# A two-layer decoder trunk with experts: one room for staged weights, fixed places for side work, a shorter split queue, and a router without GpSimd

## The chip, the cores and the metric

The kernel runs on one core of a Trainium2 chip. The metric is the time of one execution on the device in microseconds (us). Five engines work beside each other, each through its own instructions in the order in which they were written: PE (TensorE, matmuls), DVE (VectorE), ACT (ScalarE), POOL (GpSimd) and SP (SyncE, which here only issues loads). They wait for each other by semaphores. Sixteen DMA engines move the data.

## The reference

Two pre-norm layers over 256 tokens of width 1024. Each layer is an attention block and a feed-forward block; the feed-forward is a dense SwiGLU in layer 0 and a mixture of 8 experts, two for each token, in layer 1. A last RMS norm follows. All is float32.

```python
def swiglu(t, w_gate, w_up, w_down):
    return (jax.nn.silu(t @ w_gate) * (t @ w_up)) @ w_down

def moe_swiglu(h, router, w_gate, w_up, w_down):
    ...
    logits = (t @ router).astype(jnp.float32)
    top_val, top_idx = lax.top_k(logits, TOP_K)
    gates = jax.nn.softmax(top_val, axis=-1)
    combine = jnp.sum(jax.nn.one_hot(top_idx, N_EXPERTS, dtype=jnp.float32) * gates[..., None], axis=1)
    out = jnp.zeros_like(t)
    for e in range(N_EXPERTS):
        out = out + combine[:, e:e + 1].astype(t.dtype) * swiglu(t, w_gate[e], w_up[e], w_down[e])
    return out.reshape(B, S, D)
```

Each expert has three matrices of 1024 x 3584 values: 44 MB in float32, 352 MB for the eight. Each is read once.

## The kernel before

**Weights in a stream.** All weights come through one class, Stream, as a list of units in the order of use. SP loads a unit in float32 into a stage tile (load_next, L162). ACT casts it into a float16 tile, its high part `hi` (L169, scaled by 512). DVE makes the low part `lo` = stage * 512 - hi, also float16 (L172). PE then makes three float16 products: hi with the high part and the low part of the tokens, and lo with their high part. A few units are marked to be used unsplit, in float32 (L1151); each gate and each up matrix of a half ends with one. There are nine stage tiles and six pairs of hi and lo, and four more places for a stage in tiles that attention leaves free. A stage is free when its low part is made, and the next load is issued then (low_done, L192 to L199). At most eight loads are under way. The stream splits up to six units ahead of the one in use (`most`), and the split instructions are written into ACT's and DVE's order at that place.

**Experts in halves.** An expert is worked in two halves of 1792 hidden columns, 16 halves i = 0 to 15. For a half, gate_up takes 8 gate units and 8 up units of 128 x 1792 (28 or 42 matmuls each, of 128 x 96), and then the chain that makes the hidden values: for each of three column ranges, DVE multiplies silu(gate) by up (sg, L1178), ACT casts (L1179), DVE subtracts (L1180). Then down takes the 7 down units (2 x 128 rows of 1024 columns each) of the half before, i - 1. So the order of the units is gate(i), up(i), down(i-1). The last down half is split finer at its end, and its last nine units are split in two halves each (`brisk`).

**Side work.** Before an expert, its tokens (at most 96) are put in columns: slots (DVE, L1070) makes the selection, four gathers (PE L1082, then xgh by ACT and xgl by DVE L1087) and gather_last fetch them. After an expert, turn_back (L1210 to L1216) and scatter (L1218 to L1224) add its result to x. These pieces are taken from a queue, one after each up unit from the sixth on and after each down unit.

**The router.** At the end of attention of layer 1, the residual is added (x, L736). Then Plain.part squares x on ACT and multiplies it by the norm's gain on POOL (L440, four operations), PE makes the logits, DVE finds the two largest and the row scale y from the squares (L357 to L362). hh is the high part of x * gain * y, hl its low part (L1108). SP goes on issuing the experts' loads meanwhile, as far as stages are free. top_up (L1114) is called once in the middle of this and casts the next unit.

**The end.** After the last down half: finish (L1208), turn_back, scatter into x (L1224), the last norm and the output (L1265).

Of the kernel before, what the change touches and what calls it, by code (L numbers as in the profile page):

```python
# [41 lines left out]
NB = FH // P  # L42

# [26 lines left out]
def hybrid_trunk_kernel(ctx: ExitStack, tc: tile.TileContext, a: dict, out: bass.AP, dbg=None):  # L70
# [4 lines left out]
    stgp = ctx.enter_context(tc.tile_pool(name="stgp", bufs=N_STG))  # L75
    cvtp = ctx.enter_context(tc.tile_pool(name="cvtp", bufs=N_CVT))
# [30 lines left out]
    def expert_units(sets, tail=False):  # L107
# [3 lines left out]
        for i in range(len(seq) + 1):  # L111
# [4 lines left out]
            if i > 0:  # L116
                (_, _, wd), h = seq[i - 1]
                ends = tail and i == len(seq)
                got += [(rows(wd, h * FH + r * P, 2, 0, D), 2, D, False) for r in range(0, NB - 4 if ends else NB, 2)]
                if ends:  # L120
                    r0 = h * FH + (NB - 4) * P
                    got += [(rows(wd, r0 + r * P, kt, c0, 512), kt, 512, False) for r, kt, c0 in ((0, 4, 0), (0, 2, 512), (2, 2, 512))]
        return got

    MLA_KT = (2, 2, 4)
    units = []
    for layer in range(DEPTH):
# [12 lines left out]
        else:  # L140
            sets = [(a["moe_w_gate"][j, e], a["moe_w_up"][j, e], a["moe_w_down"][j, e]) for e in range(NE)]
            units += expert_units(sets, layer == DEPTH - 1)

    class Stream:


        def __init__(self, units, stage_tile, part_tiles, ahead):
            self.units, self.stage_tile, self.part_tiles = units, stage_tile, part_tiles
            self.loaded = self.split = self.low = self.used = 0
            self.stage, self.place, self.high, self.ready = {}, {}, {}, {}  # L150
# [3 lines left out]
            self.brisk = 0  # L154

        def load_next(self, place=None):
            u = self.loaded
            if u < len(self.units):
                src, kt, n, _ = self.units[u]
                stg = self.stage_tile(u, place)  # L160
                self.place[u] = place
                nc.sync.dma_start(stg[:, : kt * n].rearrange("p (k n) -> p k n", k=kt), src)  # L162
                self.stage[u] = stg
                self.loaded += 1
            elif place is None and self.last:
                self.last.pop()()
# [7 lines left out]
        def split_next(self):  # L174
# [7 lines left out]
            m = self.units[u][1] * self.units[u][2]  # L182
            self.high[u] = self.part_tiles[0](u)
            self.split += 1
            if u >= len(self.units) - self.brisk:
                self.low_until(u)
                lo = self.part_tiles[1](u)
# [8 lines left out]
        def top_up(self):  # L196

            if self.split < min(len(self.units), self.used + N_CVT) and not self.units[self.split][3]:
                u = self.split  # L199
                self.high[u] = self.part_tiles[0](u)  # L200
# [21 lines left out]
        def get(self, later=0):  # L222
            while self.split <= self.used + later:
                self.split_next()
# [1178 lines left out]
```

## Time and profile before

| | us |
|---|---|
| three runs | 1367.33, 1368.21, 1368.56 |
| median | 1368.21 |
| profiled execution | 1368.37 |
| its span | 1366.6 |
| first expert matmul | 495.03 |
| output issued | 1357.48 |

The span is what the trace covers; the execution's own time is 1.8 us longer. All times in the rows below are us from the start of the span. A row of the timeline gives start, duration, engine, line, operation, what it writes and reads, how many were merged, and in brackets the idle time of the engine before it with what ended it.

### The profile page before, as it was taken

The numbers are of one execution on the slowest core, as the hardware profiler recorded it, in microseconds if no ns is written. First come the engines' busy times: TensorE is split into PE (matmuls) and PEld (weight loads), VectorE is DVE, ScalarE is ACT, GpSimd is POOL, SyncE is SP. The second block draws the span as 40 slices with busy tenths as digits, with TensorE's granted clock in tenths as the row PEclk, the third lists the DMA queues.
The fourth block names the chain that finished last, engine by engine and source line by source line (L and its number), as shares of the span: only waits on it lengthen the run. The fifth ranks groups of instructions, "written<-read, shape, count | busy, mean of one in ns | idle before, by whom it ended". The sixth has DMA issues, their size and how long they took to land.

```text
span 1366.6 us, 43224 instructions
## 1 busy us (share of the span) xinstructions
PE 1277.3 (93%) x19680; PEld 1134.5 (83%) x19680; DVE 1079.5 (79%) x1032; ACT 898.2 (66%) x916; POOL 32.4 (2%) x51
## 2 busy tenths in 40 slices
PE   8999999999999998999999998998998998999885
PEld 5785877777587688999989988998998998999874
DVE  6655775666564587899998898898898998989976
ACT  6554654444544576788777678677777776877764
POOL 2300000000010010000000000000000000000000
PEclk9999999999999999999999999999999999999998
DMA  9953475646443459999999999999999999999991
GB/s 272 353 171 124 155 247 198 203 149 203 156 172 111 175 196 392 400 406 414 413 411 416 412 412 416 411 411 412 408 414 402 403 416 408 410 405 407 412 361 57
DMA packets 128799, 434.35 MB, mean 318 GB/s; under 512 B 11936, under 2 KB 59440, under 8 KB 128480
## 3 DMA queue, kind: packets, MB, share of 16 engines
q1 hardware_dynamic: 126640, 429.72, 81.4%
q8 instruction: 156, 2.56, 0.8%
q0 software_dynamic: 928, 1.78, 0.5%
q14 instruction: 35, 0.29, 0.1%
q10 hardware_dynamic: 1040, 0.00, 0.0%
HBM read 430.41 MB, written 1.06 MB: 316 GB/s over the span
## 4 chain that ended last, share of the span: by engine, by line
PE 23%; DMA 19%; DVE 11%; issue 5%; ACT 3%; SPq 0%; DVEq 0%; ACTq 0%
DMA stg<-in_moe_w_down_dram 13%; DVE lo L172 8%; PE my L1190 5%; DMA stg<-in_moe_w_up_dram 3%; DMA stg<-in_moe_w_gate_dram 3%; PE mu L1151 2%; PE my L1192 2%; PE mg L1161 2%; PE mg L1158 2%; PE mg L1157 2%; PE mg L1151 1%; ACT hi L169 1%; PE mu L1158 1%; PE mu L1157 1%; PE mu L1161 1%
## 5 line engine op out<-in xcount | busy, mean ns | idle before, releaser
L172 DVE SCALAR_TENSOR_TENSOR lo<-stg,hi 128x1792 f16<-128x1792 f32 (+3 forms) x418 | 849.4, 2078 | 44.0 <-ACT hi L169 43.8
L169 ACT ACTIVATE hi<-stg 128x1792 f16<-128x1792 f32 (+3 forms) x418 | 714.4, 1738 | 154.0 <-DMA stg<-in_moe_w_down_dram 56.7
L1158 PEld LDWEIGHTS <-hi 128*128 128x128 f16 x3136 | 271.8, 98 | 11.3 <-issue 11.1
L1157 PEld LDWEIGHTS <-hi 128*128 128x128 f16 x3136 | 272.7, 99 | 4.2 <-issue 4.0
L1192 PE MATMUL my<-rest,hi 128*128 128x96 f16 x1792 | 182.9, 208 | 0.9 <-issue 0.9
L1190 PE MATMUL my<-rest,hi 128*128 128x96 f16 x1792 | 183.0, 208 | 0.3 <-issue 0.3
L1190 PEld LDWEIGHTS <-hi 128*128 128x128 f16 x1792 | 157.6, 99 | 6.2 <-issue 3.3
L1192 PEld LDWEIGHTS <-hi 128*128 128x128 f16 x1792 | 157.2, 99 | 4.1 <-issue 1.0
L1157 PE MATMUL mg<-xgh,hi 128*128 128x96 f16 x1568 | 151.3, 208 | 8.0 <-DVE x L1224 6.0
L1158 PE MATMUL mg<-xgl,hi 128*128 128x96 f16 x1568 | 151.5, 208 | 5.4 <-issue 5.3
L1161 PEld LDWEIGHTS <-lo 128*128 128x128 f16 x3136 | 146.3, 98 | 5.2 <-issue 3.5
L1157 PE MATMUL mu<-xgh,hi 128*128 128x96 f16 x1568 | 147.1, 206 | 0.1
L1158 PE MATMUL mu<-xgl,hi 128*128 128x96 f16 x1568 | 147.1, 206 | 0.0
L1190 PE MATMUL my<-rest,lo 128*128 128x96 f16 x1792 | 115.4, 208 | 7.9 <-DVE lo L172 7.2
L1190 PEld LDWEIGHTS <-lo 128*128 128x128 f16 x1792 | 89.6, 99 | 9.6 <-DVE lo L172 8.6
L1161 PE MATMUL mg<-xgh,lo 128*128 128x96 f16 x1568 | 86.7, 207 | 2.9 <-issue 2.9
L1161 PE MATMUL mu<-xgh,lo 128*128 128x96 f16 x1568 | 85.2, 206 | 0.1
L459 PEld LDWEIGHTS <-hi 128*128 128x128 f16 x640 | 62.6, 98 | 9.9 <-issue 2.7
L460 PEld LDWEIGHTS <-hi 128*128 128x128 f16 x640 | 62.6, 98 | 7.2
L461 PEld LDWEIGHTS <-lo 128*128 128x128 f16 x640 | 62.6, 98 | 7.2
L1179 ACT CAST rest<-sg 128x480 f16<-128x480 f32 (+1 forms) x48 | 27.1, 566 | 60.4 <-DVE sg L1178 60.4
L1151 PE MATMUL mu<-xr,stg 128*128 128x96 f32 x448 | 64.4, 312 | 0.0
(355 smaller groups left out, 1868.2 us busy)
## 6 DMA issues: line engine op xcount, KB each, us to landing
stg<-in_moe_w_gate_dram SPq DMA_DIRECT2D x128, 896.0 KB, 17.9
stg<-in_moe_w_up_dram SPq DMA_DIRECT2D x128, 896.0 KB, 17.4
stg<-in_moe_w_down_dram SPq DMA_DIRECT2D x111, 1024.0 KB, 19.2
stg<-in_w_in_dram SPq DMA_DIRECT2D x14, 1024.0 KB, 7.0
stg<-in_dense_w_gate_dram SPq DMA_DIRECT2D x14, 1024.0 KB, 6.5
stg<-in_dense_w_up_dram SPq DMA_DIRECT2D x14, 1024.0 KB, 5.1
stg<-in_dense_w_down_dram SPq DMA_DIRECT2D x14, 1024.0 KB, 5.0
stg<-in_w_out_dram SPq DMA_DIRECT2D x8, 1024.0 KB, 9.0
```

The source lines that it names most:

```text
L169: se.activation(self.high[u][:, c], self.stage[u][:, c], AF.Copy, scale=SW)
L172: ve.scalar_tensor_tensor(lo[:, c], self.stage[u][:, c], SW, self.high[u][:, c], op0=OP.mult, op1=OP.subtract)
L459: te.matmul(ps, lh, rh, start=first, stop=False)
L460: te.matmul(ps, lh, rl, start=False, stop=False)
L461: te.matmul(ps, ll, rh, start=False, stop=last)
L1151: te.matmul(ps[b][:, c * C : (c + 1) * C], w[0][:, j * P : (j + 1) * P], xr, start=False, stop=ends and j + 1 == spans[b][1])
L1157: te.matmul(dst, L, xh[:, k, :], start=k == 0 and c == 0, stop=False)
L1158: te.matmul(dst, L, xl[:, k, :], start=False, stop=False)
L1161: te.matmul(ps[b][:, c * C : (c + 1) * C], lo[:, j * P : (j + 1) * P], xh[:, k, :], start=False, stop=ends and j + 1 == spans[b][1])
L1179: se.copy(hi[:, c], sg[:, c])
L1190: te.matmul(dst, W, L[0], start=first and part == 0 and d % 4 == 0, stop=ends and part == 1 and d % 4 == 3)
L1192: te.matmul(dst, W, L[1], start=False, stop=False)
```

## The change

The edits, in the order in which they stand:

- **One room.** The stage tiles and the pairs become one tile of 124,800 bytes for each partition, with a list of free ranges: stages are taken from below, pairs from above. Attention and the dense layer keep 9 stages and 6 pairs of the old size. Expert units take their exact size (7168 or 8192 bytes), with an edge between stages and pairs at 11 x 7168: 11 stages and 6 pairs. From half 3 on (`lean`) the edge leaves room for 4 pairs, and 11 or 12 stages stand below it.
- **A shorter split queue.** From half 3 on, three units are split ahead in place of six.
- **Fixed places.** Gathers stand at 5, 7, 9, 11 and 13 (units 0 to 7 are the up units, 8 to 14 the down units), returns at 5, 6 and 9 to 12; slots for the next expert stand at the start of the half. For half 0, slots of expert 1 and the last gather of expert 0 stand behind the third gate unit.
- **Last tiles.** The last down half comes as five units of two rows and five pieces of 512 columns; two of the former and three of the latter are used unsplit.
- **The router.** POOL has no part in it. The scale y is made ahead of the logits, and x * y * gain is one DVE operation for each of the two row tiles; hh is an ACT cast. Three of the four copies of the turned x go to ACT instead of two. top_up stands behind the gathers, and so do the first operations on the router weights (g2).

```diff
+ROOM = N_STG * 8320 + N_CVT * 8320
+EDGE = N_STG * 8320
+EDGE_X = 11 * FH * 4
+ENDS = ((0, 10, 2), (0, 12, 2), (512, 10, 2), (512, 12, 1), (512, 13, 1))
+WHOLE = (2, 6, (0, 12), (512, 10), (512, 13))
...
-                got += [(rows(wd, h * FH + r * P, 2, 0, D), 2, D, False) for r in range(0, NB - 4 if ends else NB, 2)]
+                whole = WHOLE if ends else ()
+                got += [(rows(wd, h * FH + r * P, 2, 0, D), 2, D, r in whole) for r in range(0, NB - 4 if ends else NB, 2)]
                 if ends:
-                    r0 = h * FH + (NB - 4) * P
-                    got += [(rows(wd, r0 + r * P, kt, c0, 512), kt, 512, False) for r, kt, c0 in ((0, 4, 0), (0, 2, 512), (2, 2, 512))]
+                    got += [(rows(wd, h * FH + r * P, kt, c0, 512), kt, 512, (c0, r) in whole) for c0, r, kt in ENDS]
...
+        def edge(self, u):
+            return ROOM - 4 * 8192 if self.lean else EDGE_X if u >= self.narrow else EDGE
...
-                stg = self.stage_tile(u, place)
+            if place or self.stage_tile:
+                stg = (self.stage_tile or own_tile)(u, place)
+            else:
+                got = places.take(self.size(u) * 4 if u >= self.narrow else 8320, True, self.edge(u))
+                if got is None:
+                    return False
...
-            ge.tensor_tensor(self.xg[:, t, c], x[:, t, c], self.gain[:, c], op=OP.mult)
+
+        def rows_scale(self):
+            ss = com.tile([P, NT], F32, tag="ss", name="ss_m")
+            ve.tensor_tensor(ss, self.ss[:, 0], self.ss[:, 1], op=OP.add)
+            self.y = rstd_of(ss, D, "m", NT)
...
-            if half == 0:
+            if half + t > 0:
                 se.copy(dst, src)
...
         nxt.part(1, 1)
-        nxt.turn(1, 0)
-        stream[0].top_up()
+        nxt.turn(1, 1)
+        nxt.rows_scale()
         nxt.logits(0)
...
-        se.activation(hh[:, 0, :], xgf[:, 0, :], AF.Copy, scale=y[:, 0:1])
-        top(1)
+        for t in range(NT):
+            ve.scalar_tensor_tensor(xgf[:, t, :], x[:, t, :], y[:, t : t + 1], feed.gain, op0=OP.mult, op1=OP.mult)
+            se.copy(hh[:, t, :], xgf[:, t, :])
+            top(t)
...
-        ve.tensor_scalar(hh[:, 1, :], xgf[:, 1, :], y[:, 1:2], None, op0=OP.mult)
-        for t in range(NT):
-            se.activation(xgf[:, t, :], xgf[:, t, :], AF.Copy, scale=y[:, t : t + 1])
...
+        for job in gathers(0):
+            job()
         ve.tensor_tensor(g2[:, :, 1], m8[:, :, 1], m8[:, :, 0], op=OP.subtract)
         ve.tensor_tensor(g2[:, :, 1], g2[:, :, 1], y, op=OP.mult)
         se.activation(g2[:, :, 1], g2[:, :, 1], AF.Exp)
-        for job in gathers(0):
-            job()
         stream[0].top_up()
...
+                if i == 0 and k == 2 and not tag:
+                    gather_last(0, "down")
+                    slots(1)
...
+                if i == n_half - 1 and tag == "":
+                    se.activation(sg[:, c], sg[:, c], AF.Copy, scale=SW)
...
             if i % 2 == 0 and e + 1 < NE:
-                side.append(lambda e=e: slots(e + 1))
-                side.extend(gathers(e + 1))
+                if i:
+                    slots(e + 1)
+                side.extend(zip((5, 7, 9, 11, 13), gathers(e + 1)))
             if i % 2 == 1 and e > 0:
-                side.extend(returns(e - 1))
+                side.extend(zip((5, 6, 9, 10, 11, 12), returns(e - 1)))
+            if i == 3:
+                stream[0].ahead = stream[0].most = 3
+                stream[0].lean = True
```

Two places in the program show how the instructions move. The first is ACT at the end of the router; hi76 is the unit whose low part is the first behind the router, g2 the router weights, xgh the gathered tokens. Before:

```order
L169 ACTIVATE hi76_4911<-stg76_4116 128x1792
L358 ACTIVATE y_m_4950<-v_m_4949 128x2
L359 ACTIVATE y_m_4950<-y_m_4950 128x2
L1032 ACTIVATE hh_m_4958<-xg_4863,y_m_4950 128x1024
L1048 ACTIVATE xg_4863<-xg_4863,y_m_4950 128x1024 x2
L1111 ACTIVATE g2_4964<-g2_4964 128x2
L1085 CAST xgh0_4991<-gx0_00_4999 128x384
L1085 CAST xgh0_4991<-gx0_01_5009 128x384
```

After, on the same engine at the same place (`room` is the one tile; L249 is the cast of a high part):

```order
L440 ACTIVATE y_m_4676<-v_m_4675 128x2
L441 ACTIVATE y_m_4676<-y_m_4676 128x2
L1116 CAST hh_m_4707<-xg_4623 128x1024 x2
L1166 CAST xgh0_4742<-gx0_00_4747 128x384
L1166 CAST xgh0_4742<-gx0_01_4757 128x384
L1195 ACTIVATE g2_4718<-g2_4718 128x2
L249 ACTIVATE room_58<-room_58 128x1792
L1197 ACT_TABLE_LOAD
```

The cast of the stream's unit moved from ahead of the row scale to behind the gathered tokens and the exponential of g2.

The second is DVE in half 13, around the chain of the hidden values (sg and rest, for mu13). Before, five low parts of down units (128x2048) stand ahead of it:

```order
L172 SCALAR_TENSOR_TENSOR lo380_20097<-stg380_19496,hi380_20051 128x2048
L172 SCALAR_TENSOR_TENSOR lo381_20145<-stg381_19550,hi381_20095 128x2048
L172 SCALAR_TENSOR_TENSOR lo382_20193<-stg382_19603,hi382_20143 128x2048
L1216 TENSOR_TENSOR back_4985<-yt50_20197,back_4985 96x512
L172 SCALAR_TENSOR_TENSOR lo383_20248<-stg383_19649,hi383_20191 128x2048
L1216 TENSOR_TENSOR back_4985<-yt51_20252,back_4985 96x512
L172 SCALAR_TENSOR_TENSOR lo384_20277<-stg384_19741,hi384_20246 128x2048
L1224 SCALAR_TENSOR_TENSOR x_80<-st5_00_20281,share_4967,x_80 128x512
L1178 SCALAR_TENSOR_TENSOR sg_4986<-mu13_0_19912,sg_4986 128x480
```

After, with L252 the low part, L1310 and L1318 the return's two operations, and L1267 the chain's first:

```order
L1310 TENSOR_TENSOR back_4736<-yt50_19161,back_4736 96x512
L252 SCALAR_TENSOR_TENSOR room_58<-room_58 128x2048
L1310 TENSOR_TENSOR back_4736<-yt51_19213,back_4736 96x512
L252 SCALAR_TENSOR_TENSOR room_58<-room_58 128x2048
L1267 SCALAR_TENSOR_TENSOR sg_4737<-mu13_0_18888,sg_4737 128x480
L1269 TENSOR_TENSOR rest1_4735<-sg_4737,rest_4734 128x480
L1267 SCALAR_TENSOR_TENSOR sg_4737<-mu13_1_18889,sg_4737 128x480
L1269 TENSOR_TENSOR rest1_4735<-sg_4737,rest_4734 128x480
L1267 SCALAR_TENSOR_TENSOR sg_4737<-mu13_2_18890,sg_4737 128x384
L1269 TENSOR_TENSOR rest1_4735<-sg_4737,rest_4734 128x384
L252 SCALAR_TENSOR_TENSOR room_58<-room_58 128x2048 x2
```

Two low parts of down units stand ahead of the chain now, and five behind it; the last half (i = 15) has the same order.

## Rows read from the trace of the kernel before

**Rows 1.** The page: busy time of the two busiest engines, share of the span, instructions.

```profile
PE 1277.3 (93%) x19680; PEld 1134.5 (83%) x19680; DVE 1079.5 (79%) x1032; ACT 898.2 (66%) x916; POOL 32.4 (2%) x51
```

**Rows 2.** Busy time of each engine by stretch: the stretch and its length, busy us (instructions) of PE, PEld (weight loads), DVE, ACT and POOL, granted PE clock, busy share of the DMA engines, GB/s.

```profile
500.00:1296.00 796.00, 740.65 (x15062) 726.69 (x15060) 724.02 (x476) 604.52 (x459) 0.61 (x1) 0.97 1.02 409
...
1320.00:1340.00 20.00, 20.00 (x455) 19.40 (x452) 18.11 (x20) 17.37 (x22) 0.00 (x0) 1.00 0.65 238
```

**Rows 3.** Who waited for whom from 700 to 1300 us: total us, times, longest; ACT's first group and PE's first.

```profile
ACT hi L169 <- DMA stg<-in_moe_w_down_dram: 51.3, 57, 3.3
...
PE gx L1082 <- DVE back L1070: 24.5, 5, 5.7
```

**Rows 4.** Busy time by stretch of 3 us around the router's end (the first and the last two of five; columns as in rows 2).

```profile
484.00:487.00 3.00, 3.00 (x25) 2.49 (x24) 2.42 (x6) 1.45 (x2) 2.77 (x3) 1.00 0.00 0
...
493.00:496.00 3.00, 2.76 (x33) 2.46 (x32) 2.14 (x3) 1.96 (x6) 0.00 (x0) 0.50 0.00 0
496.00:499.00 3.00, 3.00 (x63) 3.00 (x62) 2.83 (x2) 2.97 (x3) 0.00 (x0) 0.84 0.39 81
```

**Rows 5.** The load queue in order of time: start, time until the last of the group was issued, how many loads.

```profile
376.41 53.37 SPq L162 DMA_DIRECT2D stg<-in_moe_w_gate_dram  x8
439.63 39.19 SPq L162 DMA_DIRECT2D stg<-in_moe_w_up_dram  x8
496.98 13.25 SPq L162 DMA_DIRECT2D stg<-in_moe_w_gate_dram  x8
```

**Rows 6.** ACT, POOL and DVE in order of time from the router to the first resumed load (start, duration).

```profile
481.81 4.96 POOL L440 TENSOR_TENSOR xg<-x,gain 128x512 f32<-128x512 f32 x4 [9.71 <-PE wo L461]
...
483.59 1.70 ACT L169 ACTIVATE hi<-stg 128x1792 f16<-128x1792 f32 x1
485.61 1.20 DVE L357 TENSOR_SCALAR v_m<-ss_m 128x2 f32<-128x2 f32 x1
...
487.70 0.16 DVE L362 SCALAR_TENSOR_TENSOR y_m<-z_m,y_m 128x2 f32<-128x2 f32 x1
...
490.31 2.36 DVE L1108 TENSOR_TENSOR hl_m<-xg,hh_m 128x1024 f16<-128x1024 f32 x2 [0.21 <-ACT xg L1048]
...
494.42 0.56 DVE L1087 CAST xgl<-gx 128x384 f16<-128x384 f32 x1 [0.36 <-PE gx L1082]
494.90 2.02 DVE L172 SCALAR_TENSOR_TENSOR lo<-stg,hi 128x1792 f16<-128x1792 f32 x1
...
497.07 1.28 ACT L1115 ACT_TABLE_LOAD   x1
```

**Rows 7.** Busy time by stretch of 3 us behind half 0 (columns as in rows 2).

```profile
541.00:544.00 3.00, 3.00 (x71) 3.00 (x69) 1.66 (x2) 2.52 (x2) 0.00 (x0) 0.94 0.75 233
544.00:547.00 3.00, 3.00 (x75) 3.00 (x73) 3.00 (x3) 2.82 (x3) 0.00 (x0) 1.00 0.95 314
...
550.00:553.00 3.00, 3.00 (x41) 3.00 (x38) 3.00 (x3) 2.50 (x3) 0.00 (x0) 1.00 0.99 332
```

**Rows 8.** The end in order of time on ACT, PE, DVE and SP's queue (start, duration).

```profile
1303.17 1.91 ACT L169 ACTIVATE hi<-stg 128x2048 f16<-128x2048 f32 x1 [3.32 <-DMA stg<-in_moe_w_down_dram]
...
1315.86 1.91 ACT L169 ACTIVATE hi<-stg 128x2048 f16<-128x2048 f32 x1 [0.18 <-DMA stg<-in_moe_w_down_dram]
...
1313.20 1.30 PE L1222 MATMUL st<-back,peT 96*128 96x512 f16 x2 [4.96 <-ACT back L1215]
...
1319.45 0.64 DVE L1178 SCALAR_TENSOR_TENSOR sg<-mu,sg 128x480 f32<-128x480 f32 x1
...
1324.34 0.56 DVE L1180 TENSOR_TENSOR rest<-sg,rest 128x384 f16<-128x384 f32 x1 [0.58 <-ACT rest L1179]
...
1335.81 11.57 DVE L172 SCALAR_TENSOR_TENSOR lo<-stg,hi 128x1024 f16<-128x1024 f32 x12
...
1349.14 1.41 DVE L1224 SCALAR_TENSOR_TENSOR x<-st,share,x 128x512 f32<-128x512 f32 x2 [0.47 <-PE st L1222]
...
1357.48 2.69 SPq L1265 DMA_DIRECT2D out_dram<-o_main  x4
```

**Rows 9.** Groups of instructions by shape from 700 to 1300 us: busy us, mean ns of one, idle before and what ended it.

```profile
L172 DVE SCALAR_TENSOR_TENSOR lo<-stg,hi 128x1792 f16<-128x1792 f32 x159 | 309.8, 2020 | 3.2 <-ACT hi L169 3.2
...
L172 DVE SCALAR_TENSOR_TENSOR lo<-stg,hi 128x2048 f16<-128x2048 f32 x77 | 176.0, 2287 | 22.2 <-ACT hi L169 22.0
```

**Rows 10.** PE in order of time in an up unit of the last half: 28 float16 matmuls lie between the starts of the first two rows; the third is a whole unit in float32.

```profile
1302.75 0.21 PE L1157 MATMUL mu<-xgh,hi 128*128 128x96 f16 x1
...
1303.94 0.76 PE L1161 MATMUL mu<-xgh,lo 128*128 128x96 f16 x14
...
1304.97 3.26 PE L1151 MATMUL mu<-xr,stg 128*128 128x96 f32 x28
```

**Rows 11.** Busy time by stretch behind PE's wait at 1308 to 1313 us (columns as in rows 2; the third number from the end is the granted clock).

```profile
1313.00:1319.00 6.00, 5.66 (x53) 4.34 (x53) 5.81 (x5) 4.44 (x4) 0.00 (x0) 0.50 1.01 392
1319.00:1322.00 3.00, 3.00 (x57) 2.76 (x56) 2.32 (x4) 0.59 (x1) 0.00 (x0) 0.90 1.03 405
```

**Rows 12.** What the load queue waited for, from 500 to 560 and from 560 to 700 us, the first group of each: total us, times, longest.

```profile
SPq L162 <- DVE lo L172: 44.1, 20, 9.1
...
SPq L162 <- DVE lo L172: 90.5, 47, 7.1
```

More of the change, by code (lines that the diff above doesn't have):

```diff
@@ new lines, in part_tile @@
+        def part_tile(self, u, low):
+            size = self.size(u) * 2 if u >= self.narrow else 4160
+            if not low:
+                pair = places.take(2 * size, False, self.edge(u))
+                both = [(pair[0], size), (pair[0] + size, size)] if pair else [places.take(size, False, self.edge(u)) for _ in range(2)]
+                if not all(both):
+                    for got in filter(None, both):
+                        places.give(got)
+                    return None
+                self.held_by.setdefault(u, []).extend(both)
+            return at(self.held_by[u][low - 2], F16)
@@ L168, in high_part, with stage_free @@
+        def stage_free(self, u):
+            self.stage.pop(u)
+            place = self.place.pop(u)
+            if place or self.stage_tile:
+                self.load_next(place)
+            else:
+                places.give(self.held_by[u].pop(0))
+            while self.stage_tile is None and self.load_next():
+                pass
         def high_part(self, u, c):
@@ L232, in done @@
             if self.units[u][3]:
-                self.stage.pop(u)
-                self.load_next(self.place.pop(u))
+                self.stage_free(u)
+            else:
+                for got in self.held_by.pop(u):
+                    places.give(got)
             if self.later:
@@ L854, in attention @@
             if i == NHD + 1 and layer == DEPTH - 1:
[L855 removed]
+                late["gain"] = ext.tile([P, 2048], F32, tag="e1", name="gain")[:, :D]
                 ge.dma_start(late["gain"], spread(a["ffn_norm"][layer], D))
@@ L1102, in gathers @@
         def gathers(e):
-            return [lambda i=i, half=half: gather(e, i, half) for i in range(2) for half in range(2)] + [lambda: gather_last(e)]
+            last = [lambda: gather_last(e)] if e else []
+            return [lambda i=i, half=half: gather(e, i, half) for i in range(2) for half in range(2)] + last
         keep_warm(2, pw, ident16, cm16)
@@ L1150, in into @@
                     b, c = divmod(j, PER)
-                    te.matmul(ps[b][:, c * C : (c + 1) * C], w[0][:, j * P : (j + 1) * P], xr, start=False, stop=ends and j + 1 == spans[b][1])
+                    te.matmul(ps[b][:, c * C : (c + 1) * C], w[0][:, 0, j * P : (j + 1) * P], xr, start=False, stop=ends and j + 1 == spans[b][1])
             else:
@@ L1162, in into, with beside @@
             unit_done()
+        def beside(side, at):
+            while side and side[0][0] <= at:
+                side.popleft()[1]()
         def gate_up(i, e, tag, side):
@@ L1172, in gate_up @@
                 into(ps, k, e)
-                if k > 4 and side:
-                    side.popleft()()
+                beside(side, k)
             hi, lo = hTs[i % 2]
@@ L1203, in down @@
                 unit_done()
-                if side:
-                    side.popleft()()
+                beside(side, KD + r // 2)
         def finish(acc, n):
@@ L1233, in final_gain @@
         def final_gain():
-            fin["g"] = stgp.tile([P, 2080], F32, tag="stg", name="final_gain")[:, :D]
-            nc.sync.dma_start(fin["g"], spread(a["final_norm"], D))
+            got = places.take(D * 4, True, EDGE_X)
+            if got:
+                fin["g"] = at(got, F32)
+                nc.sync.dma_start(fin["g"], spread(a["final_norm"], D))
+            return got
         stream[0].last.append(final_gain)
@@ L1337, in moe @@
             else:
-                while side:
-                    side.popleft()()
+                beside(side, 99)
             assert not side
```

148 lines of the change are left out of this document (91 added, 57 removed).

## The prediction

> **What bounds the kernel now.** I read the page first: its busy shares say that PE (93%) is the bound and DVE (79%) is next [rows 1]. That is an average over stages with different limits, so the second view is the busy time by stretch. From 500 to 1296 us the DMA engines are busy all the time (share 1.02) and move 409 GB/s; DVE is busy 724 of 796 us, PE 741 [rows 2]. There the waits of ACT's casts are waits for weights: 51.3 us for the down units alone [rows 3]. So in the expert part (352 MB) the transfers end last, and the compute keeps pace with little to spare. One half of an expert is 16 units of 917,504 B and 7 of 1,048,576 B, 22.02 MB: at 409 GB/s 2.24 us a gate or up unit, 2.56 us a down unit, 53.8 us a half. Time can come out of three places: the stretch in which the DMA stands still before the first expert, dips in its rate, and what lies behind the last landing.
>
> The first: between 484 and 496 us nothing is moved [rows 4]. The queue had issued eight gate and eight up units and resumed at 496.98 [rows 5], when DVE's first lo behind the router had freed a stage: 494.90 + 2.02 = 496.92 [rows 6]. The second: at 541 to 553 the rate falls to 233, 314 and 332 GB/s [rows 7], behind a stall of PE and low parts that come late. The third: DVE's low parts run on to 1347.4, x follows at 1349.14, the output at 1357.48 [rows 8].
>
> **The change part by part.** The profiled execution took 1368.37 us for a span of 1366.6; the median is 1368.21. I make the sum on the span and add 1.6.
>
> *More stages.* The exact sizes give 11 stages in place of 9 beside the four other places. By its waits in the new order, the load queue has 18 expert units issued ahead of the router instead of 16; the two extra wait for low parts that DVE makes before the router begins. They are moved while the DMA stood idle: 2 x 2.24 = **-4.5 us**, if the transfers bound what follows. They need 4.5 of the 13 idle us, so they fit.
>
> *Router and first resume.* POOL's four products (4.96 us) end at 486.77, and DVE's v_m of 2 columns took 1.20 us beside them; y_m, of the same 2 columns, took 0.16 once POOL was done [rows 6]. Without POOL, y is ready some 2.8 us earlier (about 485.05 against 487.86). But now DVE itself makes the scaled rows, two operations of 1024 columns. The trace has no such operation; the nearest is hl, 2.36/2 = 1.18 us each [rows 6], so 2.4 us stand in DVE ahead of the slots: the saving is spent, and the gathers start within 0.4 us of where they did. What moves the DMA is another edit: the cast of the unit whose low part frees the first stage (hi, 1.70 us at 483.59 [rows 6]) now stands behind the gathers and behind the exponential of the router weights, which waits for two DVE operations behind both xgl casts. These casts end at 494.98 [rows 6]; plus about 0.1 for the two small operations' remainder and 0.2 for the exponential gives a cast from 495.1 to 496.8 and a low part to 496.85 + 2.02 = 498.9, against 496.92: **+1.9 us**. Ends: +1.2 (the gathers come 0.7 earlier) and +2.7 (the second low part, behind the table load, is the one that counts).
> The Trainium skill (GPSIMD Engine Reference, section "1. Specifications") says that GpSimd shares its SBUF interfaces with VectorE and contends with certain VectorE operations; the trace agrees with the 1.20 us. By that page alone the router would gain 1.0 us; the sum above does not use it, since the gain is spent before it reaches the DMA.
>
> *The dips at 541 to 553.* Against 409 GB/s they cost 3 x (176 + 95 + 77)/409 = 2.6 us. Two more units in stages cover 4.5 us of late low parts, but the gathers of the second expert still come in a burst at the end of half 0. Ends 0 and -2.6; I take half, **-1.3**. Other dips come at a DMA share near 1, and I take 0 for them.
>
> *The fixed places for gathers and returns.* The slots operations used to sit behind low parts in DVE, and PE's gathers waited 24.5 us for them in five times [rows 3]. This goes, but the transfers hid it: 0. If PE or DVE were the bound, it would be worth up to 24.5/11 = 2.2 us a half.
>
> *The shorter split queue (from half 3).* It takes nothing off any engine. In a half whose transfers pace the work, only two low parts of the down units now stand ahead of the sg chain in DVE, where four or five did. The chain is a ping-pong with ACT of 5.5 us (1319.45 to 1324.9 [rows 8]); a down low part takes 2.29 us, a gate one 2.02 [rows 9]. PE then has two units ready, 2 x 48 x 42.5 ns = 4.1 us (28 matmuls in 1.19 us [rows 10]), while DVE needs 5.5 + 2.3 = 7.8 for the third. So PE waits some 4 to 7 us in each half, which it did not do. DVE's own work stays 14 x 2.02 + 7 x 2.29 + 5.5 + about 1.5 of side work = 51.3 against 53.8; PE's is 14 x 42 x 42.5 ns + 2 x 3.26 + 7 x 2.04 + about 1.2 = 47. I take **0**, since 47 + 5 is under 53.8 and 15 or 16 stages buffer a late half; the price where that fails is a rival below.
>
> *The last half.* Landings of its down units pace ACT (the first cast at 1303.17, the sixth at 1315.86: 2.54 us apart [rows 8]). DVE before: five low parts, then chain, then the rest up to 1347.4. After, on the same landings and with the return's additions in between: low parts of units 0 and 1 to 1311.6, chain to 1317.1, five low parts of 2.29 and four additions of 0.7 to 1331.4, the first unit of the last down half to 1333.9. Five of the last ten pieces (r=2, r=6, and three ends) are used whole, so DVE saves 2.35 + 2.35 + 1.17 + 1.17 + 0.6 = 7.6 us (twelve half low parts took 11.57 with the smaller ones [rows 8]) and is no longer last. PE is: it gets the low part of the first unit at 1333.9, and then owes the rest of that unit and 1.9 + 2.04 + 1.9 + 2.04 + 1.02 + 0.93 + 0.93 + 0.51 = 11.3 (whole ones at 3.26/28 = 116 ns a matmul [rows 10]), some 1346.4, then turn and last piece, 1347.4. x comes at about 1348.7 against 1349.14: **-0.5**. Ends: +1 if PE is at the low clock behind its wait, and -8 (rival 1).
>
> Sum: -4.5 + 1.9 - 1.3 + 0 - 0.5 = -4.4; span 1362.2, time **1363.8 us**.
>
> **The rivals.**
> 1. *The tail gives all it can.* If PE is not held behind DVE (units 2 to 6 of half 14 are split on landing), the end follows the last landing. After 1320 some 4.8 MB are moved [rows 2], 11.6 us at 409 GB/s, so the last weights are in at about 1333 to 1336; two whole pieces and the turn add some 5 us, x at about 1341: -8 in place of -0.5, **1356**. For it: DVE is the engine that works through to the end. Against it: the order puts the chain and six 2.3-us low parts ahead of the last half's split units.
> 2. *The queue of three makes PE late in every half: slower.* PE idles behind the sg chain, and its clock falls. In the tail of before a wait of 4.96 us was followed by a granted clock of 0.50 for about 6 us (the 1.2 GHz level) and 0.90 after [rows 8, 11]: matmuls at 81 ns instead of 42.5, 3 us lost. The price is 4.9 + 3 = 7.9 us a half; PE's slack is 53.8 - 47 = 6.8, so it decides from there on. Over by 1.1 in the twelve halves 3 to 14 is +13: **1377**; a third of it gives no change. For it: the order shows the wait in each half. Against it: once late, PE finds its low parts made and does not wait.
> The Trainium skill (TensorE: Matmul & The Clock Gate, section "HAM oscillation — how this bites in real kernels") tells of a kernel that waits before each tile and so starts each one at the low clock; by that, rival 2 holds in every half. The trace agrees for one wait with 0.50 behind 4.96 us.
> 3. *The head start is not kept: no change.* If DVE or PE, not the transfers, set the pace between 500 and 1300, earlier landings only wait longer; then the later first low part (+1.9) and -0.5 at the end remain, **1369**. For it: DVE and PE are busy 91 and 93% of that stretch, and until 700 the load queue waits for low parts, 44.1 and 90.5 us [rows 12]. Against it: the DMA share is 1.02, and ACT waited for landings up to 1315 [rows 3, 8].
>
> **How the numbers follow.** Forecast 0.46, rival 1 0.14, rival 2 0.22, rival 3 0.18. A difference of 0.2% (2.7 us) is what a measurement can tell from no change. Faster 0.60 (forecast and rival 1), same 0.18 (rival 3), slower 0.22 (rival 2; its milder part counts as same, which the forecast's own misses balance). The range takes in rival 1 with a little more than its price (1354) and most of rival 2 (1375), and leaves out its last part and a tail beyond 1354. The likeliest case alone has 1360 to 1367.
>
> **What would show it.** Right: transfers last until about 488 before the router's end and resume near 499; the rate from 556 to 1296 stays at 409; the landings of the last half come about 4 us earlier; PE shows a wait for a low part behind each sg chain. Wrong: a lower GB/s and DMA share from half 3 on with PE clock dips (rival 2); landings that come earlier while x does not (rival 3 or a worse tail); x within 6 us of the last landing (rival 1).

## The result

The changed kernel takes 1382.88 us (median of four runs, 1380.16 to 1385.05), the kernel before 1368.38 in the same round: a ratio of 1.0106, 95% interval 1.0094 to 1.0118. It is 14.5 us slower, where 1363.8 was forecast with a range up to 1375. The profiled execution has a span of 1379.9 us (1366.6 before).

Busy time by stretch of the changed kernel, with the columns of [rows 2]:

```profile
540.00:560.00 20.00, 20.00 (x408) 20.00 (x407) 15.34 (x8) 13.50 (x11) 0.00 (x0) 0.96 0.74 276
...
700.00:1296.00 596.00, 548.39 (x11047) 535.61 (x11044) 535.19 (x346) 448.10 (x339) 0.00 (x0) 0.96 1.02 409
...
1320.00:1340.00 20.00, 15.74 (x276) 14.33 (x274) 17.89 (x17) 12.61 (x11) 0.00 (x0) 0.83 0.69 264
1340.00:1360.00 20.00, 20.00 (x317) 20.00 (x314) 8.49 (x9) 7.76 (x10) 0.00 (x0) 1.00 0.01 2
```

From 700 us on the transfers run at the same 409 GB/s, and they end at about the same time as before (264 GB/s from 1320 to 1340 us, 238 in [rows 2]). But from 1340 to 1360 us nothing is moved and PE is busy all the time: the weights are there, and the compute is behind them. Who waited for whom from 700 to 1300 us, in the form of [rows 3] (first ACT, then PE, then the load queue):

```profile
ACT room L249 <- PE mg L1240: 28.9, 18, 2.6
ACT room L249 <- PE my L1286: 23.6, 38, 1.6
ACT room L249 <- PE mu L1240: 22.9, 21, 1.7
ACT room L249 <- PE my L1284: 18.1, 11, 2.0
ACT room L249 <- PE mu L1243: 8.0, 11, 1.0
ACT room L249 <- PE mg L1243: 2.1, 5, 0.6
...
PE my L1284 <- DVE room L252: 41.9, 13, 4.2
...
SPq L220 <- DVE room L252: 411.8, 199, 7.2
```

In the kernel before, ACT's casts waited for landings, 51.3 us for down units alone [rows 3]. Now they wait for PE's matmuls, 103.6 us in six groups, and for no landing among the groups that count. The gathers' wait for the slots (24.5 us [rows 3]) is gone, and PE waits 41.9 us for low parts of down units instead. The load queue (SPq) waits 411.8 us for low parts to free a stage, where it waited 136.5 us in the kernel before: the stages stand full, because the compute is late.

The router, DVE and ACT in order of time, as in [rows 6]:

```profile
483.11 0.69 DVE L822 SCALAR_TENSOR_TENSOR x<-wo,x 128x512 f32<-128x512 f32 x1 [0.85 <-PE wo L547]
484.98 0.17 DVE L439 TENSOR_SCALAR v_m<-ss_m 128x2 f32<-128x2 f32 x1
486.24 1.29 DVE L1115 SCALAR_TENSOR_TENSOR xg<-x,y_m,gain 128x1024 f32<-128x1024 f32 x1
487.81 1.26 DVE L1115 SCALAR_TENSOR_TENSOR xg<-x,y_m,gain 128x1024 f32<-128x1024 f32 x1
495.95 1.68 ACT L249 ACTIVATE room<-room 128x1792 f16<-128x1792 f32 x1
497.66 2.02 DVE L252 SCALAR_TENSOR_TENSOR room<-room 128x1792 f16<-128x1792 f32 x1 [1.86 <-ACT room L249]
```

v_m takes 0.17 us in place of 1.20, now that POOL is idle. The Trainium skill (GPSIMD Engine Reference, section "1. Specifications") says that GpSimd shares its SBUF interfaces with VectorE; the trace agrees. The scaled rows cost 1.29 and 1.26 (1.18 was estimated), and the first low part ends at 499.68 (498.9 forecast, 496.92 before); 1.4 us of that is the residual's last addition, which itself comes at 483.11 instead of 481.71.

The tail in order of time, PE's last float32 up unit, the start of DVE's chain and x, as in [rows 8, 10]:

```profile
1315.33 3.26 PE L1233 MATMUL mu<-xr,room 128*128 128x96 f32 x28
...
1320.31 0.65 DVE L1267 SCALAR_TENSOR_TENSOR sg<-mu,sg 128x480 f32<-128x480 f32 x1
...
1362.41 1.41 DVE L1318 SCALAR_TENSOR_TENSOR x<-st,share,x 128x512 f32<-128x512 f32 x2 [0.47 <-PE st L1316]
```

The chain of work that ended last, its three longest pieces behind 1340 us (start, duration, what):

```profile
1343.71 3.61 PE my L1282 x32
1349.36 3.61 PE my L1282 x32
1356.03 3.61 PE my L1282 x32
```

PE's last up unit of half 15 ends at 1318.6, 10.4 us later than before (1308.2 in [rows 10]). DVE's chain (the sg row) starts only 0.9 us later than before (1320.31 against 1319.45 [rows 8]), because it stood behind five low parts then. Set against the forecast on the landings of before, which had this chain at 1311.6 and x at 1348.7, 37.1 us behind it, the chain is 8.7 us late, and x comes 42.1 us behind it: 5.0 us more. Behind 1340 us the chain that ended last runs through PE, and its longest pieces are the unsplit ones: the first two are units of two rows, each 16 matmuls in the code, and the trace shows 32 records and 3.61 us for each; the third is two of the 512-column pieces.

### The profile page after: what moved, and what is told of

The parts are those of the page before. It is cut to its first block, busy times and chain, and to the rows that moved or that the text cites. A ratio compares the mean times of both kernels' runs of the same rounds, so it can differ in the third digit from the quotient of the medians.

```text
span 1379.9 us, 43078 instructions
## 1 busy us (share of the span) xinstructions
PE 1289.2 (93%) x19625; PEld 1144.6 (83%) x19625; DVE 1074.0 (78%) x1024; ACT 892.5 (65%) x911; POOL 27.5 (2%) x47
## 4 chain that ended last, share of the span: by engine, by line
PE 44%; DVE 9%; ACT 4%; DMA 3%; issue 2%; DVEq 0%
PE my L1284 8%; DVE room L252 6%; PE mg L1243 5%; PE mg L1240 4%; PE mg L1239 4%; PE mu L1243 4%; PE mu L1239 4%; PE mu L1240 4%; PE my L1286 4%; PE mg L1233 3%; ACT room L249 2%; ACT rest L1268 1%; DVE sg L1267 1%; DMA room<-in_moe_w_gate_dram 1%; DVE rest L1269 1%
## 5 line engine op out<-in xcount | busy, mean ns | idle before, releaser
L252 DVE SCALAR_TENSOR_TENSOR room<-room 128x1792 f16<-128x1792 f32 (+4 forms) x312 | 645.8, 2098 | 89.8 <-ACT room L249 88.0
L249 ACT ACTIVATE room<-room 128x1792 f16<-128x1792 f32 (+4 forms) x312 | 542.5, 1758 | 244.2 <-issue 61.3
L1284 PE MATMUL my<-rest,room 128*128 128x96 f16 x3480 | 256.0, 214 | 50.6 <-DVE room L252 50.4
L1284 PEld LDWEIGHTS <-room 128*128 128x128 f16 x3480 | 243.7, 103 | 58.2 <-DVE room L252 53.1
L1240 PEld LDWEIGHTS <-room 128*128 128x128 f16 x3136 | 271.4, 98 | 8.0 <-issue 7.9
L1239 PEld LDWEIGHTS <-room 128*128 128x128 f16 x3136 | 272.2, 98 | 4.3 <-issue 4.0
L252 DVE SCALAR_TENSOR_TENSOR room<-stg,room 128x1792 f16<-128x1792 f32 (+2 forms) x98 | 203.9, 2096 | 10.4 <-ACT room L249 10.4
L249 ACT ACTIVATE room<-stg 128x1792 f16<-128x1792 f32 (+2 forms) x98 | 170.7, 1755 | 37.4 <-PE mg L1240 12.6
L1286 PE MATMUL my<-rest,room 128*128 128x96 f16 x1740 | 186.6, 213 | 0.0
L1286 PEld LDWEIGHTS <-room 128*128 128x128 f16 x1740 | 160.4, 102 | 4.1 <-issue 1.4
L1239 PE MATMUL mg<-xgh,room 128*128 128x96 f16 x1568 | 150.8, 208 | 7.8 <-ACT peT L1181 4.0
L1240 PE MATMUL mg<-xgl,room 128*128 128x96 f16 x1568 | 150.7, 208 | 2.7 <-issue 2.5
L1243 PEld LDWEIGHTS <-room 128*128 128x128 f16 x3136 | 146.5, 98 | 6.1 <-issue 3.4
L1240 PE MATMUL mu<-xgl,room 128*128 128x96 f16 x1568 | 147.0, 206 | 0.3 <-issue 0.3
L1239 PE MATMUL mu<-xgh,room 128*128 128x96 f16 x1568 | 146.9, 206 | 0.0
L1243 PE MATMUL mg<-xgh,room 128*128 128x96 f16 x1568 | 86.9, 207 | 2.3 <-issue 1.6
L1243 PE MATMUL mu<-xgh,room 128*128 128x96 f16 x1568 | 85.4, 206 | 0.4 <-issue 0.2
L545 PEld LDWEIGHTS <-room 128*128 128x128 f16 x640 | 62.9, 98 | 10.1 <-issue 2.7
L546 PEld LDWEIGHTS <-room 128*128 128x128 f16 x640 | 62.9, 98 | 7.5
L547 PEld LDWEIGHTS <-room 128*128 128x128 f16 x640 | 62.9, 98 | 7.6
L1268 ACT CAST rest<-sg 128x480 f16<-128x480 f32 (+1 forms) x48 | 27.1, 565 | 57.3 <-DVE sg L1267 57.3
## 6 DMA issues: line engine op xcount, KB each, us to landing
room<-in_moe_w_up_dram SPq DMA_DIRECT2D x90, 896.0 KB, 12.5
```

The costliest lines, as they stand in the source:

```text
L249: se.activation(self.high[u][:, c], self.stage[u][:, c], AF.Copy, scale=SW)
L252: ve.scalar_tensor_tensor(lo[:, c], self.stage[u][:, c], SW, self.high[u][:, c], op0=OP.mult, op1=OP.subtract)
L545: te.matmul(ps, lh, rh, start=first, stop=False)
L546: te.matmul(ps, lh, rl, start=False, stop=False)
L547: te.matmul(ps, ll, rh, start=False, stop=last)
L1239: te.matmul(dst, L, xh[:, k, :], start=k == 0 and c == 0, stop=False)
```

## The experiments

All times are medians; the ratio is to the kernel before on the same chip, with its 95% interval. An interval reaches 1.2 to 2.3 us to either side, so a difference of 1 or 2 us between two runs is not clear of noise by itself.

### The short queue, and what it acts through

**e1_long_queue.** Six units ahead to the end.

```diff
-            if i == 3:
-                stream[0].ahead = stream[0].most = 3
-                stream[0].lean = True
```

> The changed kernel without its block at half 3: six units are split ahead to the end, the edge stays at 11 gate stages. Theory Q (with three units ahead only two down low parts stand ahead of the sg chain, PE waits some 3 to 4 us behind it in each half, its clock falls, and PE becomes the bound): the end of the last up unit of half 15 comes some 8 to 10 us earlier than the 1318.6 of the changed kernel, PE's waits for low parts of down units from 700 to 1300 fall from 41.9 us to under 10, time 1371 to 1375. Theory R (the late first resume at 500.1 and the dip to 64 GB/s at 544 to 547 delay everything, the queue is innocent): 1380 or more, the last up unit still ends at 1316 or later.

1372.26 us (1.0026, 1.0014 to 1.0039): 10.6 less than the changed kernel. The last up unit ends at 1304.9, 13.7 us earlier and so more than the 8 to 10 expected. PE's waits for low parts fall to 16.7 us (under 10 was expected), and ACT waits for landings again. The block at half 3 costs some ten us; theory R falls.

**e2_three_six_pairs.** Three units ahead, but the edge and so the places for pairs as before half 3.

```diff
                 stream[0].ahead = stream[0].most = 3
-                stream[0].lean = True
```

> The changed kernel with three units ahead from half 3 on, but without the lean edge, so that the places of the pairs stay as they were (6 gate pairs). Theory Q: it is the order that makes PE wait, not the number of pairs: no change to the changed kernel, 1381 to 1385. Rival P (four pairs make ACT's casts wait for PE, and that makes the low parts late): ACT's waits for PE shrink and the time falls to 1372 to 1377.

1380.37 us (1.0092, 1.0075 to 1.0109): 2.5 less than the changed kernel, and the intervals overlap. Rival P falls: with two more pairs to hand out, ACT still waits for PE as long as in the changed kernel (102.2 us against 103.6).

**e4_before_three.** The same queue in the kernel before.

```diff
+            if i == 3:
+                stream[0].ahead = stream[0].most = 3
             if i < n_half:
                 gate_up(i, e, "", side)
```

> The kernel before with one edit: three units split ahead from half 3 on, all else as it was. Theory Q: the same wait behind the sg chain appears, 6 to 11 us slower than before, 1374 to 1379. Theory R: 1367 to 1370, since neither the resume nor the dip is touched.

1367.08 us (0.9995, 0.9985 to 1.0004): no change. Here theory Q fell, which had looked settled by e1. The order is the one that was forecast, with the chain behind two low parts, and it starts within half a microsecond of the forecast. Its first row in the last half, from DVE in order of time:

```profile
1311.18 0.64 DVE L1178 SCALAR_TENSOR_TENSOR sg<-mu,sg 128x480 f32<-128x480 f32 x1
```

Waits from 700 to 1300 us, PE's longest group and the groups of ACT's casts behind PE:

```profile
PE my L1190 <- DVE lo L172: 35.6, 19, 5.6
...
ACT hi L169 <- PE mu L1158: 0.6, 1, 0.6
ACT hi L169 <- PE mg L1161: 0.3, 1, 0.3
```

PE waits for low parts nearly as long as in the changed kernel (41.9 us), and the time doesn't show it. ACT's casts wait 0.9 us for PE, not 103.6. So the queue does harm only in the changed kernel. One thing that differs there is which place is handed out. In the kernel before, the tiles of a pair rotate among six, so a cast writes where PE read six split units ago. The room hands out the topmost free range; with three ahead, by the code, this is as a rule the one just given back, whose last reader is the matmul issued just before. Two places more (e2) change nothing in that. The next run tests it.

**e5_three_next_fit.** e2 with pairs handed out going on downward from the last one.

```diff
         def take(self, size, below, edge):
-            for a, b in self.free if below else self.free[::-1]:
-                lo, hi = (a, min(b, edge)) if below else (max(a, edge), b)
+            tops = (ROOM,) if below else (self.down, ROOM)
+            for top in tops:
+                for a, b in self.free if below else self.free[::-1]:
+                    lo, hi = (a, min(b, edge)) if below else (max(a, edge), min(b, top))
...
+                        if not below:
+                            self.down = at
```

> The changed kernel without the lean edge (as in the run with three units ahead and six places for pairs), with one edit more: the room hands out pairs going on downward from the last one given, instead of the topmost free range, which is the one that PE has just given back. Theory A (the cost of the three-unit queue is not the order behind the sg chain but the reuse: with three units ahead the topmost free range is always the pair of the unit that PE has only just finished, so ACT's cast of each unit waits for PE, and the engines work in lockstep): ACT's waits for PE matmuls from 700 to 1300 us, some 100 us in that run, nearly vanish, the last up unit of half 15 ends at 1304 to 1309 instead of 1316.2, time 1370 to 1374. Theory Q (the order with two low parts ahead of the chain): 1379 to 1382, as in that run.

1372.36 us (1.0031, 1.0020 to 1.0043): 8.0 less than e2 (8.3 by the ratios; the two ran on different chips), from which it differs only in the place that is handed out. The waits of ACT's casts in e2 from 700 to 1300 us, the four largest of six groups behind PE:

```profile
ACT room L249 <- PE mg L1240: 29.1, 20, 2.6
ACT room L249 <- PE mu L1240: 24.2, 22, 2.1
ACT room L249 <- PE my L1286: 21.7, 38, 1.4
ACT room L249 <- PE my L1284: 17.2, 11, 2.0
```

The same in e5, the largest group behind landings and the largest behind PE:

```profile
ACT room L254 <- DMA room<-in_moe_w_up_dram: 21.4, 23, 2.6
...
ACT room L254 <- PE my L1289: 4.9, 8, 0.9
```

What the load queue waits for in that stretch, in e2 and then in e5, and last PE's longest group in e5:

```profile
SPq L220 <- DVE room L252: 435.0, 199, 7.2
```

```profile
SPq L225 <- DVE room L257: 57.3, 45, 3.8
...
PE my L1289 <- DVE room L257: 39.1, 19, 4.9
```

PE's last float32 up unit of half 15, in e2 and then in e5:

```profile
1312.89 3.26 PE L1233 MATMUL mu<-xr,room 128*128 128x96 f32 x28
```

```profile
1303.33 3.26 PE L1238 MATMUL mu<-xr,room 128*128 128x96 f32 x28
```

The casts' waits for PE go from 102.2 us in all to 12.3, those for landings are back, and the last up unit ends 9.6 us earlier. DVE's waits for ACT's casts fall from 29.4 to 17.2 us, and the load queue's waits for low parts from 435.0 to 57.3. Theory A holds: the reuse of the place just freed tied ACT to PE, and through ACT the low parts and the loads. PE's own waits for low parts hardly change (41.8 us in e2, 39.1 in e5). As in e4 they are there and cost nothing that the time shows.

### The unsplit pieces

**e3_all_split.** The changed kernel with all last pieces split.

```diff
-WHOLE = (2, 6, (0, 12), (512, 10), (512, 13))
+WHOLE = ()
...
-                if i == n_half - 1 and tag == "":
-                    se.activation(sg[:, c], sg[:, c], AF.Copy, scale=SW)
```

> The changed kernel with none of the last ten pieces used whole: all are split, and the three extra ACT operations on sg go. Theory W (a float32 matmul of 128 columns by 96 costs PE 226 ns, not 116, so the five whole pieces cost PE 5.1 us more than forecast where PE is last): 3 to 5 us faster than the changed kernel, 1378 to 1380. Rival (DVE is last again once it has to split these pieces, 7.6 us of work): no change or slower, 1382 to 1386.

1376.76 us (1.0053, 1.0036 to 1.0070): 6.1 less, where 3 to 5 was expected; the rival, DVE last again, falls. The start of DVE's chain in the last half and x:

```profile
1321.55 0.65 DVE L1267 SCALAR_TENSOR_TENSOR sg<-mu,sg 128x480 f32<-128x480 f32 x1
...
1359.56 1.41 DVE L1316 SCALAR_TENSOR_TENSOR x<-st,share,x 128x512 f32<-128x512 f32 x2 [0.47 <-PE st L1314]
```

From the chain to x it is 38.0 us in place of 42.1. This length leaves out what happened ahead of the tail, which the edit doesn't touch.

**e6_long_all_split.** e1 and e3 together.

> The changed kernel with six units ahead to the end, no lean edge, and all last pieces split. If the two costs found so far (10.6 us for the short queue in this room, 6 for the whole pieces) are separate terms that add: 1365.5 to 1368. If the whole pieces cost only because PE was late already: 1371 to 1373, as with the long queue alone.

1368.67 us (0.9999, 0.9990 to 1.0009): 3.6 less than e1, and 0.7 us over the range expected for terms that add (10.6 and 6.1 would give 1366.2). The pieces cost time in a kernel that is less late, too: from the chain to x it is 32.8 us in place of 38.3.

**e8_next_fit_all_split.** e5 and e3 together.

> Three units ahead, pairs handed out going downward, and all last pieces split. Theory A with the whole pieces as a separate term: 1365 to 1368, the short queue then costs nothing. Theory Q: 1373 to 1376.

1368.46 us (0.9997, 0.9987 to 1.0007): 3.9 less than e5; from the chain to x it is 37.2 us in place of 41.9. With both terms out, the kernel is level with the one before: what is left of the change, the two further stages among it, brings nothing in all.

### The head start

**e7_early_cast.** e6 with the one cast back ahead of the row scale.

```diff
+        stream[0].top_up()
         nxt.rows_scale()
...
-        stream[0].top_up()
         se.preload_act_table_set("silu_and_others")
```

> As the kernel with six units ahead and all pieces split, with the one cast of the stream (top_up) put back to where it stood, ahead of the row scale, instead of behind the gathers and the exponential. Theory D (the transfers bound what follows, so an earlier first resume is worth what it brings forward): the first load behind the router is issued at 497 to 498.5 instead of 500.1, and the time falls by 1 to 3 us against that kernel. Rival (the dip at 541 to 553 takes it back, or the cast delays the row scale): within 0.7 us of it.

1370.32 us (1.0011, 1.0001 to 1.0021): 1.65 more than e6, not less, a result that neither side expected. The intervals overlap; but the ten runs of each, taken on one chip in the same rounds, have means 1.5 us apart, with an interval of 1.0 to either side. The two traces differ by 1.3 us before the router, so times are counted from the start of the residual's last addition (481.83 in e7, 483.09 in e6). The first expert matmul comes 13.8 us after it (495.65), where it came 12.5 after it in e6 (495.60). The first load behind the router gains 0.6 (497.86, or 16.0 after it, against 499.72, or 16.6). So the cast brings the load a little forward and puts the expert's matmuls back; the reason shows more plainly in e11 below.

**e9_even_stages.** e8 with all expert stages of one size.

```diff
-EDGE_X = 11 * FH * 4
+EDGE_X = 10 * 8192
...
-                got = places.take(self.size(u) * 4 if u >= self.narrow else 8320, True, self.edge(u))
+                got = places.take(8192 if u >= self.narrow else 8320, True, self.edge(u))
```

> Three units ahead, pairs handed out going downward, all last pieces split, and in addition every expert stage takes 8192 bytes (ten of them) instead of its exact size (eleven of 7168). Theory F (the head start of two units is lost because a down unit of 8192 bytes doesn't fit a hole that a gate unit of 7168 leaves, so the load queue stands before the down units at 538 to 551 us while stages are free): the rate from 540 to 560 us rises from 300 to 360 GB/s or more, the seven down loads there are issued evenly, and the time falls by 2 to 4 us against the same kernel with exact sizes, 1364.5 to 1366.5. Rival L (the queue stands there because the low parts themselves come late): the dip stays, 1367 to 1370.

1365.60 us (0.9977, 0.9968 to 0.9986), the only kernel here that is faster than the one before; against e8 by their ratios 0.9977/0.9997, about 2.7 us. The load queue of e8 in order of time (the places `stg` are those outside the room):

```profile
527.67 18.54 SPq L225 DMA_DIRECT2D stg<-in_moe_w_down_dram  x3
547.78 5.50 SPq L225 DMA_DIRECT2D room<-in_moe_w_down_dram  x4
553.37 1.75 SPq L225 DMA_DIRECT2D room<-in_moe_w_gate_dram  x3
```

The same of e9:

```profile
526.84 1.69 SPq L225 DMA_DIRECT2D room<-in_moe_w_down_dram  x2
537.68 0.37 SPq L225 DMA_DIRECT2D stg<-in_moe_w_down_dram  x1
540.74 0.37 SPq L225 DMA_DIRECT2D room<-in_moe_w_down_dram  x1
543.34 0.37 SPq L225 DMA_DIRECT2D stg<-in_moe_w_down_dram  x1
545.27 2.31 SPq L225 DMA_DIRECT2D room<-in_moe_w_down_dram  x2
```

Busy time from 540 to 560 us, of e8 and then of e9 (columns as in [rows 2]):

```profile
540.00:560.00 20.00, 20.00 (x416) 20.00 (x414) 15.82 (x9) 14.62 (x11) 0.00 (x0) 0.97 0.83 300
```

```profile
540.00:560.00 20.00, 20.00 (x429) 20.00 (x427) 16.89 (x10) 17.22 (x13) 0.00 (x0) 1.00 1.02 412
```

In e8, with exact sizes, no down unit goes into the room until 547.78, and then four do, and gate units right behind them. By the code, single holes of 7168 bytes don't take 8192, and the queue is in order. With even sizes they go out as the low parts free them, and the dip is gone: 412 GB/s, where the kernel before had 361 over the same 20 us. The eight kernels with exact sizes have 265 to 338. Besides the sizes, e9 has ten expert stages in place of eleven.

**e10_nine_even.** e6 with nine even stages.

> Six units ahead, pairs from the top, all last pieces split, and nine stages of 8192 bytes: as many as the kernel before has. Theory F: the dip is no deeper than in the kernel before (361 GB/s from 540 to 560 us) in spite of two stages fewer, and the time is that of before or up to 2 us under it, 1366 to 1369. Rival L: with fewer stages the dip is deeper than with eleven (286 GB/s) and the time is 2 to 4 us longer than with eleven, 1370.5 to 1373.

1369.29 us (1.0002, 0.9993 to 1.0012): in neither of the expected ranges, and not told apart from e6 (1368.67). Its rate from 540 to 560 us is 412 GB/s where e6 has 286, with two stages fewer, so the dip came from the sizes; rival L falls for this pair. But the time doesn't show it. Perhaps two stages fewer take what the dip gives back; no run shows that. The time fell only with even sizes, a tenth stage, the shorter queue and the going-down places together.

**e11_even_early.** e9 with the early cast.

> As the kernel with ten even stages, with the one cast of the stream put back ahead of the row scale. If the first resume now counts, since the dip no longer hides it: 1 to 2 us faster than that kernel, 1363 to 1365. If it doesn't: within 0.7 us of it.

1368.03 us (0.9993, 0.9983 to 1.0003): 2.4 more than e9 (the means of their runs lie 2.3 apart, with an interval of 1.4 to either side), and neither outcome that was expected. Here the residual's last addition starts at nearly the same time in both traces (482.42 in e9, 482.34 in e11). The row scale's first DVE operation behind ACT and the first expert matmul, in e9 and then in e11:

```profile
484.97 0.16 DVE L447 TENSOR_TENSOR z_m<-y_m 128x2 f32<-128x2 f32 x1 [0.50 <-ACT y_m L446]
...
494.27 0.24 PE L1244 MATMUL mg<-xgh,room 128*128 128x96 f16 x1 [0.77 <-DVE xgl L1173]
```

```profile
486.42 0.16 DVE L447 TENSOR_TENSOR z_m<-y_m 128x2 f32<-128x2 f32 x1 [2.04 <-ACT y_m L446]
...
496.17 0.24 PE L1244 MATMUL mg<-xgh,room 128*128 128x96 f16 x1 [0.65 <-DVE xgl L1174]
```

The cast (1.71 us) stands in ACT ahead of y_m, so the row scale comes 1.45 us later and the first expert matmul 1.9 us later, while the first load behind the router is issued at the same time (498.4 in both). The rate from 540 to 560 us is 357 GB/s again, with even sizes: with the compute later the low parts free their stages later, so the sizes are not the only thing that makes the dip. Both kernels with the early cast are slower than their partners.

## Why the prediction was wrong

**What bounds the kernel: right for before, not carried over.** The transfers pace the kernel before, and the changed kernel had the same rate. The prediction took as a given that the compute stays able to keep up. In the changed kernel it doesn't: the stages stand full, and x comes more than 20 us behind the last landing.

**The shorter queue, taken as 0: the step that failed.** It was costed by the order alone. The order and the wait behind the chain came as forecast, and in the kernel before they cost nothing (e4), so the 0 was right for them. Rival 2's mechanism is not the cause: the wait is there and is made up in e4, and it is still there in e5 (39.1 us), which is 8.0 us faster. That its 1377 lies nearest to the time measured is luck. In the changed kernel the wait of 4.2 us that ends at 1112.5 is followed by a granted clock of 0.60, between the levels of 1.2 and 2.4 GHz, for one stretch of 4 us and 1.00, the upper level, from then on:

```profile
1108.00:1112.00 4.00, 0.28 (x7) 0.13 (x4) 3.42 (x4) 2.85 (x3) 0.00 (x0) 0.97 1.02 418
1112.00:1116.00 4.00, 3.49 (x45) 3.24 (x46) 4.00 (x4) 1.98 (x2) 0.00 (x0) 0.60 1.00 407
1116.00:1120.00 4.00, 4.00 (x91) 3.76 (x88) 4.00 (x3) 3.18 (x3) 0.00 (x0) 1.00 1.02 386
```

The Trainium skill (TensorE: Matmul & The Clock Gate, section "HAM oscillation — how this bites in real kernels") tells of waits that put PE back to the low clock before each tile. The trace agrees for this wait and for another of 4.2 us that ends at 1003.8, with 0.50, the lower level, from 1004 to 1008 us; by e4 and e5 it isn't what decides here.

What was left out is the place: the room gives the next pair the bytes that PE has only just read, so with three units ahead the casts wait for PE, 103.6 us in 104 waits from 700 to 1300 us. It costs 8.0 us by e2 and e5; the whole block at half 3 costs 10.6 by the changed kernel and e1.

**The last half, -0.5: mis-sized.** The start of DVE's chain behind two low parts was right, as e4 shows (1311.18, 1311.6 forecast). The price of the unsplit pieces was half of what it is: 116 ns stood for a matmul, but the row [rows 10] holds two records for each matmul of the code, 14 in 28. A two-row unit is 3.61 us and not 1.9; the first four of the five pieces cost PE 10.8 us and not 5.7, 5.2 us more than forecast. Measured in the time: 3.6 (e1 to e6), 3.9 (e5 to e8), 6.1 (changed kernel to e3). Measured from the chain to x in the traces, in the same order: 5.5, 4.7 and 4.1. The low clock that the forecast named as an end of +1 is there as well (granted clock 0.60 from 1326 to 1330 and 0.55 to 1334 us in the changed kernel, behind PE's wait at the chain); what it cost is not measured by itself.

**More stages, -4.5, and the dips, -1.3: not realized.** The units were loaded early, 18 of them ahead of the router as forecast, and the dip then was deeper: 276 GB/s from 540 to 560 us against 361. That the exact sizes leave holes which no down unit fits was not seen; e9 shows it, and takes 2.7 us back, which puts it 3.1 us under the kernel before. That rival 3 was partly right, and the compute's start counts as much as the landings here, is argued from e7 and e11 and not shown by itself: the matmuls start 1.3 and 1.9 us later there, and the time is 1.65 and 2.4 us longer.

**Router, +1.9.** The first low part ends at 499.68 instead of 498.9; counted from the residual's last addition, which came 1.4 us later, it is 0.6 early. But the first resume was the wrong quantity to look at, and the term has the wrong sign: with the cast back in its old place, where it holds up the row scale, the kernel is 1.65 (e7) and 2.4 us (e11) slower.

**The sum.** 19.1 us lie between 1363.8 and 1382.9: the queue in the room 8.0 to 10.6, the unsplit pieces 3.6 to 6.1, and the gain of 4.4 that the whole sum was to bring and that e8, with both of these out, doesn't have. These make 16.0 to 21.1. The ends don't separate better: e3 and the changed kernel were run four times each, and by the tail's length in the traces the pieces are not dearer in the kernel where PE is late.

**Still open.** What the lean edge costs by itself (2.5 us, within the intervals); where the rest of the gain of 4.4 went that e9 doesn't have; and why e10, whose rate has no dip, is not faster than e6, which has two stages more and the dip.

## What to carry to other kernels

A planner that hands out memory decides who waits for whom: first fit from one end gives each writer the bytes with the youngest reader, and a short queue then turns into lockstep, where a rotating pool of the same size does not. Sizes that differ by an eighth in one room cost more here in holes than they saved in bytes, since the load queue is in order. Before pricing an operation by a row of the trace, count the records that one instruction of the code leaves.

## What the runs showed of the hardware

A float32 matmul of 128 x 128 by 96 columns shows as two records and takes 226 ns (3.61 us for 16), against 42.5 ns for each of the three float16 products that replace it [rows 10]: unsplit work frees DVE and ACT, and costs PE 1.8 times as much.
